# One f32r product a head for the relative-bias tables of a hybrid decoder layer

## The chip, the core and the metric

The kernel runs on one core of a Trainium2 chip. The metric is the device time of one execution in microseconds, as the median of several runs. A core has TensorE (PE; its weight loads are listed as PEld), VectorE (DVE), ScalarE (ACT), GpSimd (POOL) and SyncE (SP, whose queue issues all of this kernel's DMAs). Each engine runs its own instructions in a fixed order and waits on semaphores for the others.

## The reference

One decoder layer over 16 meta tokens and 1,024 tokens with 1,024 features: a norm and an input projection, four heads of differential attention beside four heads of a gated linear recurrence, an output projection, and a convolutional feed-forward part. The change concerns the bias of the attention scores alone:

```python
dist = q_pos[:, None] - k_pos[None, :]
bias = jnp.moveaxis(rel_table.astype(f32)[rel_bucket(dist)], -1, 0)
s = jnp.einsum('bhmqd,bhmkd->bhmqk', qblk, kh).astype(f32) * scale + bias[None, :, None]
s = jnp.where(dist >= 0, s, -jnp.inf)
```

`rel_table` has 32 buckets and 4 heads. The bucket depends on the distance alone, and all distances beyond a limit share one bucket, so a score needs its own bias only near the diagonal.

## The kernel before

All products that are to be exact are made in one of two ways. In plain f32, the program issues one matmul and the profile shows two records of it. Or an operand is split into a high part in f32r, a 4-byte type of reduced precision for TensorE, and a low part, also f32r, which is the rest; the projections multiply high by high, high by low and low by high (L203, L205, L207 in `proj_step`, and L847 in the first blocks). Writing a tile of type F32R rounds, and the rest is found by a subtraction.

The first 60 us do the following. The tokens come in blocks (`xt`), are scaled by their norm on DVE (`xs`, which needs the statistic `ss` of ACT), turned by PE (L242, into `px`) and split into `ahi` and `alo`. Beside that, PE makes the query, key and value projections of head 0 (`pi_dq`, `pi_dk`, `pi_dv`) for three groups of blocks. `smalls` and `lam_terms` make small vectors. The last group, `head0(2)`, is interleaved with `bias_tables`, which yields after each head, so that the four table products lie some 4 us apart among the projections.

`bias_tables` makes, for each head, 128 equal rows of 384 values: the bias at the distances 255 down to -128. The one-hot matrix `oh` (32 buckets by 384 distances, an input) is multiplied by `tbb`, which holds the 32 table values of a head, each repeated 128 times. The product of 128x384 goes to a bank `pb` in PSUM. DVE copies it to `rb`, subtracts its first column, POOL fills the last 128 columns with a large negative number, and SP stores it to `rsc` in DRAM. There is one `rb` buffer, so each head's copy waits until the store before has landed. `attn` then loads `rr` from `rsc` with a row step of 383, which shifts each row by one distance.

The order of PE's instructions is that of the program. On the other engines a scheduler sets it when the program is built. Each DMA waits for the one that held its lane before; lanes are taken in turn. The weights of the next stage (`wr_hf`, `wr_hq`, `wr_hi`, `wr_hg`, three buffers in all) are loaded by the same SP queue, split by ACT (`wh_...`) and POOL (`wl_...`). The next stage begins with the projection `pi_hf` and reuses the SBUF space of these first steps, for `kr` among others.

Most operations on DVE, ACT and POOL go through a helper, so that the profile gives L54 as their line; they are told apart by their tiles.

Of the kernel before, what the change touches and what calls it, by code (L numbers as in the profile page):

```python
# [9 lines left out]
F32 = mybir.dt.float32  # L10
F32R = mybir.dt.float32r
U8 = mybir.dt.uint8
AF = mybir.ActivationFunctionType
ALU = mybir.AluOpType
# [3 lines left out]
P = 128  # L18
# [7 lines left out]
HEADS = 4  # L26
# [60 lines left out]
def layer_kernel(ctx: ExitStack, tc: tile.TileContext, x, meta, table, lbl, gpre, gpost, win,  # L87
# [3 lines left out]
    V, A = Ordered(tc, nc.vector, state), Ordered(tc, nc.scalar, state)  # L91
    G = Ordered(tc, nc.gpsimd, state)
    T, SY = nc.tensor, nc.sync

    def pool(name, bufs, side="left", space=None):
        kw = {"side": side} if space is None else {"space": space}
        cm = tc.tile_pool(name=name, bufs=bufs, reuse_waits="tile", **kw)
        return cm, cm.__enter__()
# [42 lines left out]
    def ps_m(name):  # L141
        return pp.tile([P, 512], F32, tag="m", name=name, bufs=deep["m"])
# [43 lines left out]
    z_cm, zp = pool("pre", 2, "right")  # L186
# [105 lines left out]
        V.tensor_scalar(nlam, nlam, -(0.8 - 0.6 * math.exp(0.0)), None, ALU.add)  # L292

    def bias_tables():
        oh = zp.tile([32, 384], F32, tag="oh", name="oh", bufs=1)
        SY.dma_start(oh, onehot)
        tb = zp.tile([32, HEADS], F32, tag="tb", name="tb", bufs=1)
        SY.dma_start(tb, table)
        tbb = zp.tile([32, HEADS, P], F32, tag="tbb", name="tbb", bufs=1)
        V.tensor_copy(tbb, tb.rearrange("b (h o) -> b h o", o=1).to_broadcast([32, HEADS, P]))  # L300
        for h in range(HEADS):
            pt = ps_m(f"pb{h}")
            T.matmul(pt[:, :384], tbb[:, h], oh, start=True, stop=True)
            rb = zp.tile([P, 384], F32, tag="rb", name=f"rb{h}", bufs=1)
            V.tensor_copy(rb, pt[:, :384])
            V.tensor_scalar(rb[:, :256], rb[:, :256], rb[:, 0:1], None, ALU.subtract)
            G.memset(rb[:, 256:], NEG)
            SY.dma_start(rsc[h].rearrange("(p c) -> p c", p=P), rb)
            yield
# [604 lines left out]
    with tc.issue_after(last_lo.ins):  # L914
        smalls()
        lam_terms()
    interleave(head0(2), [bias_tables()], 2600)
    close(z_cm, p_cm)
    p_cm, pp = pool("ps", 2, space=PSUM)
# [722 lines left out]
```

## Time and profile before

| | |
|---|---|
| median of 3 runs | 1322.26 us (1322.09 to 1323.52) |
| the profiled execution | 1325.6 us |
| its span | 1323.8 us |
| granted TensorE clock, mean | 0.997 |
| busy: PE, DVE, ACT, POOL | 97%, 70%, 52%, 34% |

In a row of the timeline stand the start in us, the busy time, the engine, the line, the operation, the tile written and the tiles read, their shapes and the count; in brackets the idle time before it and what ended that. "SPq" is the issuing of a DMA. Ends of matmuls are modelled and overlap the next one, so the step from start to start is what a product costs PE. A stretch of the table of windows gives, after its length, the busy time and count of PE, PEld, DVE, ACT and POOL.

### The profile page before, as it was taken

What the parts mean: (1) busy time and instruction counts of PE and PEld (TensorE: products, weight loads), DVE (VectorE), ACT (ScalarE), POOL (GpSimd) and SP (SyncE); (2) the same over time, 40 slices, a digit from 0 to 9 for tenths busy, and PEclk for the clock granted to TensorE, in tenths of its full rate; (3) what the DMA queues carried; (4) which work ended last, traced back from release to release, by engine and by line L of the source; (5) the groups of instructions that cost most, each with busy time, mean ns of one, the idle gap of its engine ahead of it and who ended that gap; (6) DMA issues with size and microseconds to landing.
All of it is one profiled execution on the core that took longest, in us unless ns stands there. A gap on an engine that the chain in (4) does not pass through costs nothing.

```text
span 1323.8 us, 26191 instructions
## 1 busy us (share of the span) xinstructions
PE 1286.8 (97%) x10172; PEld 1185.5 (90%) x10172; DVE 930.1 (70%) x1531; ACT 692.5 (52%) x1635; POOL 455.4 (34%) x340
## 2 busy tenths in 40 slices
PE   8999999999999999899999999999999999999997
PEld 7899999899999988677999999999999997888875
DVE  6464646465645564547997788989989967697586
ACT  8475466547544754246754444444444435454553
POOL 5211211121112111243077667676676730010121
PEclk9999999999999999999999999999999999999999
DMA  5111121112111335487232234545445428865363
GB/s 209 61 40 33 54 57 41 49 46 65 44 42 41 88 101 169 153 277 254 81 112 80 80 95 154 177 144 173 154 144 166 144 84 275 312 205 166 88 206 120
DMA packets 99427, 165.00 MB, mean 125 GB/s; under 512 B 10035, under 2 KB 34899, under 8 KB 99302
## 3 DMA queue, kind: packets, MB, share of 16 engines
q1 hardware_dynamic: 99302, 163.32, 37.8%
q8 instruction: 80, 1.31, 0.4%
q14 instruction: 45, 0.37, 0.1%
HBM read 122.65 MB, written 40.63 MB: 123 GB/s over the span
## 4 chain that ended last, share of the span: by engine, by line
PE 45%; DVE 11%; ACT 3%; issue 3%; DMA 2%; POOL 0%; SPq 0%; DVEq 0%; ACTq 0%; POOLq 0%
PE pd L1491 5%; PE pd L1492 5%; PE pd L1490 5%; DVE c L54 5%; PE pb L1316 4%; PE pb L1317 3%; PE pb L1318 3%; PE pa L1316 2%; PE pa L1317 2%; PE pa L1318 2%; PE pc L1316 2%; PE pc L1317 2%; PE pc L1318 2%; PE py L976 1%; PE py L972 1%
## 5 line engine op out<-in xcount | busy, mean ns | idle before, releaser
L1316 PE MATMUL pb<-t,uh 128*128 128x258 f32 x504 | 144.0, 286 | 8.9 <-DVE u L54 8.9
L1318 PE MATMUL pb<-t,ul 128*128 128x258 f32 x504 | 141.6, 281 | 0.0
L1317 PE MATMUL pb<-t,uh 128*128 128x258 f32 x504 | 141.6, 281 | 0.0
L1491 PE MATMUL pd<-wl,gh 128*128 128x512 f32 x308 | 122.0, 396 | 1.2 <-DVE wl L54 1.1
L1492 PE MATMUL pd<-wh,gl 128*128 128x512 f32 x308 | 121.7, 395 | 0.0
L1490 PE MATMUL pd<-wh,gh 128*128 128x512 f32 x308 | 121.7, 395 | 0.0
L54 POOL TENSOR_TENSOR c<-c,c 128x514 f32<-128x514 f32 (+1 forms) x44 | 75.2, 1709 | 121.1 <-ACT c L54 111.4
L1316 PEld LDWEIGHTS pb<-t,uh 128*128 128x128 f32 x504 | 95.4, 189 | 12.2 <-DVE u L54 12.1
L54 DVE SCALAR_TENSOR_TENSOR c<-uu,cwt,c 128x514 f32<-128x514 f32 (+1 forms) x88 | 89.2, 1023 | 19.3 <-ACT c L54 19.0
L1317 PEld LDWEIGHTS pb<-t,uh 128*128 128x128 f32 x504 | 95.6, 190 | 0.0
L1318 PEld LDWEIGHTS pb<-t,ul 128*128 128x128 f32 x504 | 95.2, 189 | 0.0
L1316 PE MATMUL pa<-t,uh 128*128 128x258 f32 (+1 forms) x336 | 95.2, 283 | 0.0
L1318 PE MATMUL pa<-t,ul 128*128 128x258 f32 (+1 forms) x336 | 95.0, 283 | 0.0
L1317 PE MATMUL pa<-t,uh 128*128 128x258 f32 (+1 forms) x336 | 94.8, 282 | 0.0
L1316 PE MATMUL pc<-t,uh 128*128 128x258 f32 (+1 forms) x336 | 94.4, 281 | 0.0
L1317 PE MATMUL pc<-t,uh 128*128 128x258 f32 (+1 forms) x336 | 94.0, 280 | 0.0
L1318 PE MATMUL pc<-t,ul 128*128 128x258 f32 (+1 forms) x336 | 93.7, 279 | 0.0
L54 DVE SCALAR_TENSOR_TENSOR c<-ug,cwt,c 128x514 f32<-128x514 f32 (+1 forms) x88 | 89.6, 1019 | 0.9 <-ACT c L54 0.6
L54 ACT CAST uh<-ra 128x512 fp32r<-128x512 f32 x67 | 41.0, 616 | 66.4 <-PE pb L1317 48.2
L1491 PEld LDWEIGHTS pd<-wl,gh 128*128 128x128 f32 x308 | 57.7, 187 | 16.5 <-DVE wl L54 2.7
L54 POOL TENSOR_TENSOR ul<-ws,uh 128x512 fp32r<-128x512 f32 x42 | 64.7, 1541 | 20.4 <-ACT uh L54 20.4
L1492 PEld LDWEIGHTS pd<-wh,gl 128*128 128x128 f32 x308 | 57.7, 187 | 14.4 <-DVE gl L54 0.4
(373 smaller groups left out, 4161.2 us busy)
## 6 DMA issues: line engine op xcount, KB each, us to landing
ra<-in_wup_dram SPq DMA_DIRECT2D x88, 256.0 KB, 3.0
mp<-msc SPq DMA_DIRECT2D x23, 512.0 KB, 6.0
wd<-in_wdown_dram SPq DMA_DIRECT2D x44, 256.0 KB, 3.3
tsc<-wd SPq DMA_DIRECT2D x44, 256.0 KB, 3.2
wi<-tsc SPq DMA_DIRECT2D x44, 256.0 KB, 2.9
gi<-gsc SPq DMA_DIRECT2D x33, 256.0 KB, 4.1
wi<-in_wdown_dram SPq DMA_DIRECT2D x33, 256.0 KB, 5.3
gsc<-c SPq DMA_DIRECT2D x22, 257.0 KB, 2.3
```

What stands on the lines that cost most here:

```text
L54: ins = call(*args, **kw)
L972: T.matmul(py[:r], mh, hi, start=(first and k == ks[0]), stop=False)
L976: T.matmul(py[:r], ml, hi, start=False, stop=(last and k == ks[-1]))
L1316: T.matmul(pt, hi[:, s], th[:, k], start=(first and k == 0), stop=False, skip_group_check=True)
L1317: T.matmul(pt, hi[:, s], tl[:, k], start=False, stop=False, skip_group_check=True)
L1318: T.matmul(pt, lo[:, s], th[:, k], start=False, stop=(k == 3), skip_group_check=True)
L1490: T.matmul(py, gh[:, s], wh, start=(k == 0 and pr not in (3, 7)), stop=False, skip_group_check=True)
L1491: T.matmul(py, gh[:, s], wl, start=False, stop=False, skip_group_check=True)
L1492: T.matmul(py, gl[:, s], wh, start=False, stop=(k == NH - 1), skip_group_check=True)
```

## The change

The 32 table values become 64 rows: the f32r rounding of the values in rows 0 to 31, and what the rounding left out in rows 32 to 63. The one-hot matrix stands twice below itself, in f32r (its zeros and ones are exact). One product over 64 rows adds the two halves. For this, the one-hot matrix and the table are each loaded twice, the former into a plain f32 tile `ohr` that takes the buffer of `rb`; ACT copies it to f32r; DVE writes `tbb` over 64 rows as f32r and then overwrites rows 32 to 63 with the difference.

```diff
     def bias_tables():
-        oh = zp.tile([32, 384], F32, tag="oh", name="oh", bufs=1)
-        SY.dma_start(oh, onehot)
-        tb = zp.tile([32, HEADS], F32, tag="tb", name="tb", bufs=1)
-        SY.dma_start(tb, table)
-        tbb = zp.tile([32, HEADS, P], F32, tag="tbb", name="tbb", bufs=1)
-        V.tensor_copy(tbb, tb.rearrange("b (h o) -> b h o", o=1).to_broadcast([32, HEADS, P]))
+        oh = zp.tile([64, 384], F32R, tag="oh", name="oh", bufs=1)
+        raw = zp.tile([P, 384], F32, tag="rb", name="ohr", bufs=1)[:64]
+        tb = zp.tile([64, HEADS], F32, tag="tb", name="tb", bufs=1)
+        for l in range(2):
+            SY.dma_start(raw[32 * l:32 * l + 32], onehot)
+            SY.dma_start(tb[32 * l:32 * l + 32], table)
+        tbb = zp.tile([64, HEADS, P], F32R, tag="tbb", name="tbb", bufs=1)
+        A.copy(oh, raw)
+        tbr = tb.rearrange("b (h o) -> b h o", o=1)
+        V.tensor_copy(tbb, tbr.to_broadcast([64, HEADS, P]))
+        V.tensor_tensor(tbb[32:], tbr[32:].to_broadcast([32, HEADS, P]), tbb[32:].bitcast(F32), op=ALU.subtract)
         for h in range(HEADS):
             pt = ps_m(f"pb{h}")
             T.matmul(pt[:, :384], tbb[:, h], oh, start=True, stop=True)
```

The order of PE stays as it is. On DVE the two instructions stand among those of the small terms, ahead of the scaling `xs` of block 6:

```order
 L54 TENSOR_TENSOR lv<-lv 128x64
-L54 COPY tbb<-tb 32x512
+L54 COPY tbb<-tb 64x512
 L54 TENSOR_REDUCE le<-lv 128x1
+L54 TENSOR_TENSOR tbb<-tb,tbb 32x512
 L54 TENSOR_SCALAR xs_427<-xt_171,ss_428,gb 128x512 x2
```

The copy is wider, and the subtraction is new, behind a reduction of `lam_terms`. In SP's queue, the loads for the tables stand between those of the small vectors and the first weights of the next stage; before:

```order
L296 DMA oh<-in_onehot_dram 32x384
L298 DMA tb<-in_table_dram 32x4
L156 DMA wr_hf_0_726<-in_win_dram 128x512
L156 DMA wr_hf_1_732<-in_win_dram 128x512
L156 DMA wr_hq_0_738<-in_win_dram 128x512
```

and after:

```order
L299 DMA ohr<-in_onehot_dram 32x384
L300 DMA tb<-in_table_dram 32x4
L299 DMA ohr<-in_onehot_dram 32x384
L300 DMA tb<-in_table_dram 32x4
L156 DMA wr_hf_0_731<-in_win_dram 128x512
L156 DMA wr_hf_1_737<-in_win_dram 128x512
L156 DMA wr_hq_0_743<-in_win_dram 128x512
```

Two loads are added. Later in the same queue, the stores of the second to fourth table (`rsc`) alternate with weight loads; before:

```order
L308 DMA rsc<-rb_619 128x384
L156 DMA wr_hi_0_934<-in_win_dram 128x512
L308 DMA rsc<-rb_648 128x384
L156 DMA wr_hi_1_940<-in_win_dram 128x512
L156 DMA wr_hg_0_1147<-in_win_dram 128x512
L308 DMA rsc<-rb_679 128x384
```

and after:

```order
L313 DMA rsc<-rb_624 128x384
L156 DMA wr_hi_0_939<-in_win_dram 128x512
L156 DMA wr_hi_1_945<-in_win_dram 128x512
L313 DMA rsc<-rb_653 128x384
L156 DMA wr_hg_0_1152<-in_win_dram 128x512
L313 DMA rsc<-rb_684 128x384
```

The third table's store changes places with the load of `wr_hi_1`. With it, the third table's memset moves behind the split `wl_hq_0` on POOL, and on DVE the fourth table's copy moves behind the two `kl`. On ACT the copy of the one-hot matrix is added, ahead of the first copy to `avn`. Behind the four tables the order of every engine is the same as before.

## The prediction

> **What bounds the kernel now.** I read the page first, then the busy time in stretches, then the timeline of each engine round the bias tables, because all that the change touches lies in the first 60 us.
>
> ```profile
> span 1323.8 us, 26191 instructions
> ...
> PE 1286.8 (97%) x10172; PEld 1185.5 (90%) x10172; DVE 930.1 (70%) x1531; ACT 692.5 (52%) x1635; POOL 455.4 (34%) x340
> ...
> PE 45%; DVE 11%; ACT 3%; issue 3%; DMA 2%; POOL 0%; SPq 0%; DVEq 0%; ACTq 0%; POOLq 0%
> ```
>
> PE is busy for 97% of the span, and it holds most of what the page can place of the chain that ended last. The stretch table (busy time of PE, PEld, DVE, ACT, POOL, each with its count, then clock, DMA share and rate) says whether that holds where the tables are made:
>
> ```profile
> 42.36:59.62 17.26, 17.26 (x85) 14.05 (x85) 6.13 (x13) 6.20 (x12) 7.22 (x10) 1.00 0.35 114
> 59.62:460.00 400.38, 395.85 (x3884) 381.36 (x3883) 227.90 (x520) 229.57 (x675) 71.12 (x72) 1.00 0.17 49
> ```
>
> From 42.36 to 59.62 us, where the four table products stand between projections, PE is never idle, at full clock, and DVE, ACT and POOL work about a third of the time. In the 400 us behind it PE idles 4.5 us in all. So PE time saved before 59.62 moves everything behind it, unless a wait of another engine takes its place.
>
> The timeline of PE shows what a table product costs. L303 is the product; its "x2" are two records, since a plain f32 product runs as two. L203, L205 and L207 are projections in f32r, one record each.
>
> ```profile
> 42.19 0.34 PE L205 MATMUL pi_dv<-alo,w 128*128 128x384 f32 x1
> 42.36 0.34 PE L207 MATMUL pi_dv<-ahi,w 128*128 128x384 f32 x1
> 42.63 0.91 PE L303 MATMUL pb<-oh,tbb 32*128 32x384 f32 x2
> 43.47 0.45 PE L203 MATMUL pi_dq<-ahi,wh_dq 128*128 128x384 f32 x1
> 43.75 0.34 PE L205 MATMUL pi_dq<-alo,wh_dq 128*128 128x384 f32 x1
> ...
> 54.74 0.34 PE L207 MATMUL pi_dv<-ahi,w 128*128 128x384 f32 x1
> 55.00 0.91 PE L303 MATMUL pb<-oh,tbb 32*128 32x384 f32 x2
> 55.84 0.45 PE L203 MATMUL pi_dv<-ahi,w 128*128 128x384 f32 x1
> 56.12 0.34 PE L205 MATMUL pi_dv<-alo,w 128*128 128x384 f32 x1
> ```
>
> Busy times overlap here, so starts are what counts. Between f32r neighbours a 384-column product takes 0.17 to 0.18 us from start to start (42.19 to 42.36); I use 0.175. Round L303 the three steps from 42.36 to 43.75 take 1.39 us, and from 54.74 to 56.12 1.38 us, where three f32r steps would take 0.525. The excess has two parts: the two f32 records, and a stop at each end (42.36 to 42.63 is 0.27, not 0.175; 43.47 to 43.75 is 0.28).
>
> **The change part by part.**
>
> *The product on PE.* Four heads take 4 x 1.385 = 5.54 us now. If the single f32r product over 64 rows steps like its neighbours, they take 4 x 0.525 = 2.10, a gain of 3.44 us. Whether the stops go too is the open term, since no f32r product with fewer than 128 rows is in the trace. The nearest rows are products on other parts of the array:
>
> ```profile
> 66.30 0.34 PE L207 MATMUL pi_hf<-ahi,wl_hf 128*128 128x384 f32 x1
> 66.57 0.18 PE L670 MATMUL pt<-ident,pb 16*16 16x16 f32 x1
> 66.68 0.44 PE L203 MATMUL pi_hf<-ahi,wh_hf 128*128 128x384 f32 x1
> 66.96 0.33 PE L205 MATMUL pi_hf<-alo,wh_hf 128*128 128x384 f32 x1
> ...
> 135.36 0.28 PE L205 MATMUL pi_dq<-alo,wh_dq 128*128 128x272 f32 x1
> 135.57 0.73 PE L399 MATMUL pd<-hq,kr 128*32 128x32 f32 x62
> ...
> 535.60 0.39 PE L974 MATMUL py<-wol,mp 128*128 128x512 f32 x1
> 535.83 0.40 PE L976 MATMUL py<-woh,mp 128*128 128x512 f32 x1
> 536.07 0.40 PE L972 MATMUL py<-woh,m 128*2 128x512 f32 x1
> 536.30 0.40 PE L974 MATMUL py<-wol,m 128*2 128x512 f32 x1
> ```
>
> L670 (16 rows) and L399 (32 weight columns), both plain f32, are entered with the same stop: 0.27 us behind a 384-column step, 0.21 behind a 272-column one, against 0.175 and 272/384 of it, 0.124. L972 also uses a strip of the array (2 weight columns), but in f32r, and is entered without any: 0.24 and 0.23 against 0.23. So either the stop belongs to plain f32 on a part of the array, and goes; or it belongs to a part of the rows, and stays. The end of the bound where it stays comes from L670: 0.66 us from 66.30 to 66.96 with 16 columns, plus 368/384 of 0.175 = 0.17 for the other columns, is 0.83. The weight loads of the same rows differ:
>
> ```profile
> 66.57 0.08 PEld L670 LDWEIGHTS pt<-ident,pb 16*16 16x16 f32 x1 [0.26 <-issue]
> 66.68 0.19 PEld L203 LDWEIGHTS pi_hf<-ahi,wh_hf 128*128 128x128 f32 x1
> ```
>
> If a full load of 0.19 shows in place of the 0.08, it is 0.94. That is a gain of 0.45 to 0.56 per head, 1.8 to 2.2 us in all. I take 3.4: L399 and L972 are alike in tile and differ in type, which is just what the change alters.
>
> *DVE.* The copy of the table becomes a cast over 64 rows, and a subtraction over 32 rows is added behind it.
>
> ```profile
> 16.43 1.50 DVE L54 CAST w<-X_in 128x512 fp32r<-128x512 f32 x1
> ...
> 24.15 0.69 DVE L54 TENSOR_TENSOR alo<-px,ahi 128x512 fp32r<-128x512 f32 x1 [0.32 <-ACT ahi L54]
> ...
> 27.39 0.41 DVE L54 COPY tbb<-tb 32x512 f32<-32x512 f32 x1
> ...
> 29.47 1.41 DVE L54 SCALAR_TENSOR_TENSOR xs<-xt,ss,gb 128x512 f32<-128x512 f32 x2 [1.54 <-ACT ss L54]
> ```
>
> The cover is the 1.54 us for which DVE waits for ss of ACT in front of xs. A cast taken at 0.75 (half of the row at 16.43, the only f32r cast of this size on DVE, made beside POOL work, while POOL is idle at 27.39) adds 0.34, the subtraction 0.69: 1.03 us, hidden, with 0.5 to spare. With 1.50 for the cast and twice 0.69 for the subtraction it is 2.5 us, 0.9 past the cover; xs feeds the transposes of PE at 30.37, which wait as long. So 0 to +0.9 us; I take 0.
>
> *ACT.* The copy of the one-hot matrix, 64x384, is queued behind the two Exp of the small terms and ahead of avn.
>
> ```profile
> 33.60 0.52 ACT L54 COPY avn<-pn_va 16x128 f32<-16x128 f32 x2 [0.24 <-PE pn_va L319]
> 35.45 0.59 ACT L54 CAST ahi<-px 128x512 fp32r<-128x512 f32 x1 [1.34 <-PE px L242]
> ```
>
> At no more than the 0.59 of the 128x512 cast it fills the 0.24 and pushes avn by 0.35, which the 1.34 us wait ahead of ahi takes up: nothing. Without that cover it would cost PE 0.35.
>
> *SP and the DMAs.* Two more small loads stand ahead of the first weights of the next stage.
>
> ```profile
> 17.67 0.33 SPq L296 DMA_DIRECT2D oh<-in_onehot_dram  x1
> 19.13 0.33 SPq L298 DMA_DIRECT2D tb<-in_table_dram  x1
> 19.55 0.84 SPq L156 DMA_DIRECT2D wr_hf<-in_win_dram  x2
> ...
> 46.20 0.62 ACT L54 CAST wh_hf<-wr_hf 128x512 fp32r<-128x512 f32 x1
> ```
>
> At 1.46 us each (17.67 to 19.13) they move wr_hf to 22.5 at the latest; it is read at 46.20. Nothing.
>
> *The order behind the tables.* The memset of the third table now stands behind a weight split of POOL, its store behind a weight load of SP, and the fourth table's copy behind kl on DVE. The names end in rsc, which head 0 reads first, and in the freeing of the one rb buffer.
>
> ```profile
> 53.00 1.29 POOL L54 TENSOR_TENSOR wl_hq<-wr_hq,wh_hq 128x512 fp32r<-128x512 f32 x1 [0.20 <-ACT wh_hq L54]
> ...
> 58.05 0.33 SPq L308 DMA_DIRECT2D rsc<-rb  x1
> ...
> 63.61 0.40 ACT L54 ACTIVATE kr<-pi_hf 128x272 f32<-128x272 f32 x1
> ```
>
> The four stores of rb take this long from issue to landing:
>
> ```profile
> DMA to landing us min/median/max: 2.4/2.4/2.4
> ```
>
> With PE ahead by 1.7 us at the third table, that split ends near 52.6, so the memset and the store stay near where they are, and the last store, now at 58.05, leaves by about 57 and has landed at 59.4. The first big tile of the next stage, kr, may share the space of rb and would be written at 60.2 instead of 63.61, so 0.8 us are left. Nothing; if that margin were gone, the late part would hold ACT, and PE only behind it. What is next late is again PE.
>
> Sum: 3.4 us off the span, 1323.8 to 1320.4. The profiled execution took 1325.6, 1.8 outside the span, so it would read 1322.2. The median of the three runs, 1322.26, lies 3.3 below that execution; the same 3.4 off it gives 1318.9.
>
> **The rivals.**
>
> *The stops stay* (gain 1.8 to 2.2, middle 2.0: 1320.3). For it: L303 itself and L670, the only row-limited products, both stop. Against it: L399 stops with all 128 rows, and L972 does not. The Trainium skill, on the page TensorEngine Tiling, section Key Properties, says that a change of tiling mode, not merely of tile, drains TensorE. By that rule the gain would be this rival's; L303 agrees with it (0.27 us in place of 0.175), L972 does not (0.24 in place of 0.23).
>
> *The product does not get cheaper* (1322.3, up to 1323.2 with the 0.9 of DVE): 64 rows in f32r could run at the f32 pace. L972 speaks against it, at the full f32r step on a strip.
>
> *The second loads land late, and the kernel is slower.* DVE takes its work in order, so the cast of the table holds up xs, and xs holds up PE. The loads go out by 22.0 us at 1.46 apart. The cover is gone when the table lands after about 28.0 (29.47 less the 1.44 of cast and subtraction); from there each us costs PE one, and from 31.4 on the 3.4 us gain is used up. A landing at 35 us gives 1322.26 - 3.4 + 7.0 = 1325.9. Against it: from 22.0 to 28.0 are 6.0 us for a load of half a kilobyte.
>
> **How the numbers follow.** Forecast 0.55, stops stay 0.30, no cheaper 0.08, late loads 0.07. About 0.2%, 2.6 us, is what a measurement of this kernel can tell from no change, and the three runs span 1.4 us. The forecast's 3.4 is beyond 2.6 in about five of six cases, the 2.0 in one of four: faster 0.55 x 0.84 + 0.30 x 0.25 = 0.54; slower 0.07; the rest, 0.39, within. The range runs from 1317.7 (1.2 below the forecast, for the spread of runs) to 1321.7 (the small end of the gain with stops, 1320.5, and the same spread); it leaves out the last two rivals and the tails, 0.19.
>
> **What would show it.** In the changed profile: one record a table product; the three steps round it at 0.53 us if I am right, at 0.8 to 0.95 if the stops stay, near 1.4 if it is no cheaper. The first hf projection starts near 56.2 in place of 59.62 (57.6 with stops), and PE stays without idle time up to there. At 30.4 the transposes must not wait for xs. If all that holds and the span has not shrunk by as much, the gain was lost behind 60 us, which I hold for unlikely because all orders there stay as they are.

## The result and the profile after

| | before | after |
|---|---|---|
| median, 22 runs each | 1322.33 us (1321.17 to 1324.61) | 1320.38 us (1318.45 to 1323.21) |
| the profiled execution | 1325.6 us | 1319.7 us |
| its span | 1323.8 us | 1317.9 us |

The changed kernel takes 0.9985 of the time before (95% interval 0.9979 to 0.9992), 1.95 us less. The interval ends below 1, so that is faster, at about half of the forecast gain; the gain is less than the 2.6 us that the prediction took as the least that can be told from no change.

The page after (span; busy time of each engine) shows the same bound:

```profile
span 1317.9 us, 26191 instructions
...
PE 1282.9 (97%) x10168; PEld 1183.6 (90%) x10168; DVE 933.3 (71%) x1532; ACT 693.2 (53%) x1636; POOL 456.4 (35%) x340
```

PE has four records fewer, one for each table product. The timeline of PE after, round the first table product (now L308) and at the first projection of the next stage:

```profile
42.42 0.34 PE L207 MATMUL pi_dv<-ahi,w 128*128 128x384 f32 x1
42.69 0.44 PE L308 MATMUL pb<-oh,tbb 64*128 64x384 f32 x1
43.05 0.45 PE L203 MATMUL pi_dq<-ahi,wh_dq 128*128 128x384 f32 x1
43.34 0.34 PE L205 MATMUL pi_dq<-alo,wh_dq 128*128 128x384 f32 x1
...
57.76 0.29 PE L203 MATMUL pi_hf<-ahi,wh_hf 128*128 128x272 f32 x1
```

The two records have become one, but the stops are still there: the three steps take 0.27, 0.36 and 0.29 us (42.42 to 42.69, to 43.05, to 43.34), where a plain step is 0.175. The three steps from L207 to L205 take 0.92 us; over the four heads they are 0.92, 0.93, 0.91 and 0.91, 3.67 us in all, where it was 5.54. That is a gain of 1.87. The first hf projection starts at 57.76 in place of 59.62, 1.86 us earlier.

The weight loads of the same place show what a stop is:

```profile
42.24 0.19 PEld L207 LDWEIGHTS pi_dv<-ahi,w 128*128 128x128 f32 x1
42.68 0.18 PEld L308 LDWEIGHTS pb<-oh,tbb 64*128 64x128 f32 x1 [0.25 <-issue]
43.05 0.19 PEld L203 LDWEIGHTS pi_dq<-ahi,wh_dq 128*128 128x128 f32 x1 [0.18 <-issue]
```

The load for L207 starts at 42.24, 0.18 us ahead of its matmul, under the one before. The load for the table product starts at 42.68, together with its matmul, after 0.25 us in which the loader did nothing; the load for the L203 behind it waits in the same way. So going into the table product and coming out of it, PE gives up the overlap of load and matmul.

In the stretches between the table products and behind them (busy time and count of PE, PEld, DVE, ACT, POOL, then clock, DMA share and rate), PE stays the bound:

```profile
42.42:57.76 15.34, 15.34 (x82) 13.56 (x81) 6.95 (x12) 6.19 (x12) 6.26 (x9) 1.00 0.39 115
57.76:460.00 402.24, 397.70 (x3896) 383.15 (x3896) 230.80 (x525) 230.81 (x678) 71.96 (x74) 1.00 0.17 49
...
545.00:550.00 5.00, 5.00 (x30) 4.30 (x30) 0.99 (x3) 1.11 (x3) 0.00 (x0) 1.00 0.00 0
```

It is never idle up to 57.76, and idles 4.54 us from there to 460, against 4.53 before from 59.62 on. What was gained at the tables is carried on whole.

The two profiled spans differ by 5.9 us, three times as much. I don't put the rest down to the change: it arises behind 460 us, where the order of both programs is the same, and one part of it can be seen in the same stretch of the execution before:

```profile
545.00:550.00 5.00, 5.00 (x27) 3.47 (x26) 2.29 (x4) 0.58 (x1) 0.00 (x0) 0.66 0.30 108
```

Its granted clock fell to 0.66 there. Runs of one kernel lie some us apart (the table above): the execution profiled before lies 3.3 us above the median of its kernel, the one after 0.7 below. So one pair of profiles cannot tell 2 us; the medians of 22 runs can, and their 1.95 agrees with the 1.87 of the steps.

### The profile page after: what moved, and what is told of

Its sections match the earlier page's. It is cut to its first block, busy times and chain, and to the rows that moved or that the text cites. A ratio compares the mean times of both kernels' runs of the same rounds, so it can differ in the third digit from the quotient of the medians.

```text
span 1317.9 us, 26191 instructions
## 1 busy us (share of the span) xinstructions
PE 1282.9 (97%) x10168; PEld 1183.6 (90%) x10168; DVE 933.3 (71%) x1532; ACT 693.2 (53%) x1636; POOL 456.4 (35%) x340
## 4 chain that ended last, share of the span: by engine, by line
PE 45%; DVE 10%; issue 3%; ACT 2%; DMA 2%; POOL 1%; SPq 0%; DVEq 0%; ACTq 0%; POOLq 0%
PE pd L1496 5%; PE pd L1497 5%; PE pd L1495 5%; DVE c L54 4%; PE pb L1321 4%; PE pb L1322 4%; PE pb L1323 4%; PE pa L1321 2%; PE pa L1323 2%; PE pa L1322 2%; PE pc L1321 2%; PE pc L1322 2%; PE pc L1323 2%; PE py L981 1%; PE py L977 1%
```

## Experiments

The theory after the result: a product that uses fewer than the 128 rows of the array stops PE on the way in and out, whatever its type, and plain f32 costs more on top. The rivals: the stop depends on the type (and 64 rows in f32r have some other cost), it depends on how few rows there are, or it is nothing but the weight load standing free. The experiments e1 to e4 were timed beside the kernel before, whose median over 32 runs was 1321.83 us there; e5 and e6 were run once each and are read from the steps alone.

**e1: 128 rows, f32r.** The changed kernel with rows 64 to 127 of both operands filled with zeros:

```diff
-        oh = zp.tile([64, 384], F32R, ...)
-        raw = zp.tile([P, 384], F32, tag="rb", name="ohr", bufs=1)[:64]
-        tb = zp.tile([64, HEADS], F32, ...)
+        oh = zp.tile([P, 384], F32R, ...)
+        raw = zp.tile([P, 384], F32, tag="rb", name="ohr", bufs=1)
+        tb = zp.tile([P, HEADS], F32, ...)
+        G.memset(raw[64:], 0.0)
+        G.memset(tb[64:], 0.0)
...
-        tbb = zp.tile([64, HEADS, P], F32R, ...)
+        tbb = zp.tile([P, HEADS, P], F32R, ...)
...
-        V.tensor_copy(tbb, tbr.to_broadcast([64, HEADS, P]))
-        V.tensor_tensor(tbb[32:], ...)
+        V.tensor_copy(tbb, tbr.to_broadcast([P, HEADS, P]))
+        V.tensor_tensor(tbb[32:64], ...)
```

> The changed kernel with its 64 rows filled up to 128 by rows of zeros in both operands, so that the f32r product covers the whole array. Rows theory (a product over fewer than 128 rows makes PE stop on entry and on exit, whatever its type): the three steps round a table product fall from 0.92 to about 0.53 us, the first hf projection starts near 56.2 us in place of 57.76, and the time is 1.5 us below the changed kernel and 3.4 below the one before (ratio 0.9974). Lone-product theory (any single product with operands of its own between projections stops PE, rows or not): the steps stay at 0.92 and the time at the changed kernel's.

The timeline of PE in e1 (the table product is L310):

```profile
42.58 0.34 PE L207 MATMUL pi_dv<-ahi,w 128*128 128x384 f32 x1
42.76 0.34 PE L310 MATMUL pb<-oh,tbb 128*128 128x384 f32 x1
42.93 0.34 PE L203 MATMUL pi_dq<-ahi,wh_dq 128*128 128x384 f32 x1
43.11 0.33 PE L205 MATMUL pi_dq<-alo,wh_dq 128*128 128x384 f32 x1
...
56.40 0.29 PE L203 MATMUL pi_hf<-ahi,wh_hf 128*128 128x272 f32 x1
```

and of its weight loads:

```profile
42.59 0.19 PEld L310 LDWEIGHTS pb<-oh,tbb 128*128 128x128 f32 x1
42.76 0.19 PEld L203 LDWEIGHTS pi_dq<-ahi,wh_dq 128*128 128x128 f32 x1
```

The three steps take 0.53 us, a table product steps like any projection, and its load runs under the matmul before. In the product nothing but the number of rows differs from the changed kernel, so the stops belong to the rows. The time is 1318.61 us (10 runs), 0.9977 of before (0.9968 to 0.9987): 3.2 us less, about what the prediction expected of the change itself. The two memsets on POOL cost nothing that shows. By median it is the fastest of the kernels here. It is faster than the kernel before; that it is faster than the changed kernel is shown by the steps alone, since the two intervals (0.9968 to 0.9987 here, 0.9979 to 0.9992 there) overlap.

**e2: 128 rows, plain f32.** The kernel before with its 32 rows filled up to 128 with zeros:

```diff
-        oh = zp.tile([32, 384], F32, ...)
-        tb = zp.tile([32, HEADS], F32, ...)
+        oh = zp.tile([P, 384], F32, ...)
+        tb = zp.tile([P, HEADS], F32, ...)
+        G.memset(oh, 0.0)
+        G.memset(tb, 0.0)
+        SY.dma_start(oh[:32], onehot)
+        SY.dma_start(tb[:32], table)
...
-        tbb = zp.tile([32, HEADS, P], F32, ...)
+        tbb = zp.tile([P, HEADS, P], F32, ...)
```

> The kernel before, in plain f32, with its 32 rows filled up to 128 by zeros; neither split nor f32r. Rows theory: the stops go and the two f32 records stay, so the three steps take 0.175 on entry, about 0.66 for the two records, and 0.26 for the step behind (as behind the plain f32 products of the value step in the profile before), 1.1 us in place of 1.39: 1.1 us less than before in all (ratio 0.9992). Type theory, on which the forecast rested (the stop belongs to plain f32 on a part of the array): the same 1.1, since the part is gone. Lone-product theory: 1.39 as before.

The timeline of PE in e2:

```profile
42.43 0.34 PE L207 MATMUL pi_dv<-ahi,w 128*128 128x384 f32 x1
42.60 0.81 PE L305 MATMUL pb<-oh,tbb 128*128 128x384 f32 x2
42.95 0.63 PE L203 MATMUL pi_dq<-ahi,wh_dq 128*128 128x384 f32 x1
43.42 0.34 PE L205 MATMUL pi_dq<-alo,wh_dq 128*128 128x384 f32 x1
```

0.99 us for the three steps, where 1.1 was expected. L305 is entered after 0.17, without a stop, though it is plain f32. What is above 0.525, 0.465, is the price of plain f32: the two records take 0.35 from start to start, and the step behind them 0.47 in place of 0.175. With 32 rows the same product took 1.385, so the rows cost 0.395 there. The time, 1320.86 us (11 runs), is 0.9991 of before (0.9982 to 1.0000), which agrees with the expected 0.9992; the interval reaches 1, so the time alone does not settle it, and the steps do.

**e3: 32 rows, f32r.** The changed kernel with the high halves alone; the low halves of the table are left out, so it computes less:

```diff
-        oh = zp.tile([64, 384], F32R, ...)
-        tb = zp.tile([64, HEADS], F32, ...)
-        for l in range(2): ...
-        tbb = zp.tile([64, HEADS, P], F32R, ...)
+        oh = zp.tile([32, 384], F32R, ...)
+        tb = zp.tile([32, HEADS], F32, ...)
+        SY.dma_start(raw, onehot)
+        SY.dma_start(tb, table)
+        tbb = zp.tile([32, HEADS, P], F32R, ...)
...
-        V.tensor_tensor(tbb[32:], ...)
```

> The f32r product over 32 rows: the low halves of the table values are left out, so this part of the bias is only as precise as f32r. Type alone is changed against the kernel before. Rows theory: 0.92 us for the three steps, as with 64 rows, and the changed kernel's time. Type theory: 0.53. If the stop grows with the number of rows that are loaded or not loaded, it differs from 0.92.

The timeline of PE in e3:

```profile
42.34 0.34 PE L207 MATMUL pi_dv<-ahi,w 128*128 128x384 f32 x1
42.61 0.43 PE L305 MATMUL pb<-oh,tbb 32*128 32x384 f32 x1
42.98 0.44 PE L203 MATMUL pi_dq<-ahi,wh_dq 128*128 128x384 f32 x1
43.26 0.34 PE L205 MATMUL pi_dq<-alo,wh_dq 128*128 128x384 f32 x1
```

0.92 us, as with 64 rows: 32 rows stop PE no more than 64 do, and f32r doesn't spare it. Its time, 1321.23 us (11 runs), 0.9993 (0.9984 to 1.0003), settles nothing, since the interval holds both no change and the 0.9985 of the changed kernel; the steps do.

With these, the three steps round a table product are:

| rows | plain f32 | f32r |
|---|---|---|
| 32 | 1.385 (before) | 0.92 (e3) |
| 64 | | 0.92 (after) |
| 128 | 0.99 (e2) | 0.53 (e1) |

The two costs add up: 0.39 for 32 or 64 rows in place of 128, in either type, 0.465 for plain f32 at either number of rows.

**e4: the four products together.** The changed kernel with the four products issued back to back, ahead of the loop:

```diff
+        pts = [ps_m(f"pb{h}") for h in range(HEADS)]
+        for h in range(HEADS):
+            T.matmul(pts[h][:, :384], tbb[:, h], oh, start=True, stop=True)
         for h in range(HEADS):
-            pt = ps_m(f"pb{h}")
-            T.matmul(pt[:, :384], tbb[:, h], oh, start=True, stop=True)
+            pt = pts[h]
```

> The changed kernel with its four table products one behind the other, ahead of the first of the projections between which they stood. Rows theory (the cost is that of changing between 64 and 128 rows, not that of the product): one entry and one exit in place of four, so from the projection before to the second one behind about 0.92 + 3 x 0.18 = 1.45 us, and 1.2 us less than the changed kernel in all (ratio to before 0.9976). If each product pays for itself: four times what it pays now, no gain on the changed kernel.

The timeline of PE in e4 (one row for all four products):

```profile
42.31 0.34 PE L207 MATMUL pi_dv<-ahi,w 128*128 128x384 f32 x1
42.58 0.96 PE L308 MATMUL pb<-oh,tbb 64*128 64x384 f32 x4
43.47 0.45 PE L203 MATMUL pi_dq<-ahi,wh_dq 128*128 128x384 f32 x1
43.76 0.34 PE L205 MATMUL pi_dq<-alo,wh_dq 128*128 128x384 f32 x1
```

From L207 to L205 there are 1.45 us for six steps, which at 0.175 would take 1.05: one pair of stops, 0.40, instead of four. A row of products of the same kind doesn't stop between them, so it is the change between kinds that costs, and not the free-standing load of each. The time is 1319.02 us (11 runs), 0.9977 (0.9968 to 0.9986).

**e5 and e6: a strip of the columns.** The prediction had argued from column strips. e5 is e1 with one more product in front of each table product, over all 128 rows but with 32 weight columns; e6 is the same in plain f32:

```diff
             pt = ps_m(f"pb{h}")
+            T.matmul(pt[:32, :384], tbb[:, h, :32], oh, start=True, stop=True)                                   # e5
+            T.matmul(pt[:32, :384], tbb[:, h, :32].bitcast(F32), oh.bitcast(F32), start=True, stop=True)         # e6
             T.matmul(pt[:, :384], tbb[:, h], oh, start=True, stop=True)
```

> The kernel with 128 rows, with one more f32r product ahead of each table product: the same operands, but 32 weight columns in place of 128; its result is written over. Rows alone stop PE: four steps at 0.175, so 0.70 us from the projection ahead to the second one behind. A strip of columns stops it as a strip of rows does (and 2 weight columns were an exception): about 0.92 + 0.175 = 1.1 us.

> The same with the added product of 32 weight columns in plain f32. Type matters for columns (as the entry of the 32-column products of the recurrence in the profile before was read): a stop at each end, 1.39 + 0.175 = 1.56 us. Rows alone stop PE, and that entry has another cause, such as the short products themselves: 0.99 + 0.175 = 1.17 us.

The timeline of PE in e5 (L310 is the strip, L311 the table product):

```profile
42.19 0.34 PE L207 MATMUL pi_dv<-ahi,w 128*128 128x384 f32 x1
42.36 0.34 PE L310 MATMUL pb<-oh,tbb 128*32 128x384 f32 x1
42.54 0.34 PE L311 MATMUL pb<-oh,tbb 128*128 128x384 f32 x1
42.72 0.34 PE L203 MATMUL pi_dq<-ahi,wh_dq 128*128 128x384 f32 x1
42.89 0.33 PE L205 MATMUL pi_dq<-alo,wh_dq 128*128 128x384 f32 x1
```

and in e6:

```profile
42.51 0.34 PE L207 MATMUL pi_dv<-ahi,w 128*128 128x384 f32 x1
42.78 0.83 PE L310 MATMUL pb<-oh,tbb 128*32 128x384 f32 x2
43.54 0.44 PE L311 MATMUL pb<-oh,tbb 128*128 128x384 f32 x1
43.82 0.34 PE L203 MATMUL pi_dq<-ahi,wh_dq 128*128 128x384 f32 x1
44.00 0.34 PE L205 MATMUL pi_dq<-alo,wh_dq 128*128 128x384 f32 x1
```

In f32r the strip is one more step of 0.175 and nothing else: 0.70 us from L207 to L205. In plain f32 it is entered after 0.27, and the second step behind it takes 0.28; the four steps take 1.49 us, near the 1.56 expected with stops and far from the 1.17 without. So on 32 columns the stop does hang on the type, and such a strip has it in plain f32 alone; on rows it does not. In one run each beside 1321.56 us of the kernel before, e5 took 1320.07 us and e6 1320.77.

## Why the prediction was right or wrong

The time, 1320.38 us, lies in the range and on the forecast's side. It is the time of the rival in which the stops stay (1320.3), not of the likeliest case (1318.9). So the range held because it was drawn wide enough to take in that rival, to which the prediction gave a chance of 0.30, and not because the mechanism it held for likeliest was right.

*The step that failed* is "I take 3.4: L399 and L972 are alike in tile and differ in type". The pair was read rightly, and e5 and e6 show that on 32 columns the type decides. What failed is the carrying over from columns to rows: the rows of the profile had no f32r product with fewer than 128 rows, and after, e1, e2 and e3 show that the stop goes with the rows in both types. L670 and L303, which use few rows, were the nearer ones. On this the Trainium skill, on the page TensorEngine Tiling, section Key Properties, had the rule that a change of tiling mode drains TensorE: after, e3 and e4 agree with it (0.39 us for the way in and the way out together); e5 agrees only if a strip of 32 columns in f32r is no change of mode, which no run here shows (0.70 us for four steps, entered without a stop).

*The size of the rival* was right: 0.92 us for the three steps, within the forecast 0.83 to 0.94, and 1.87 us in all, within 1.8 to 2.2. Of the two ends, the full weight load was the better one, as the 0.18 of the load at 42.68 shows.

*That the gain would be carried on whole* was right: PE has no idle time up to 57.76 and as much as before behind it.

*DVE* was right that it is hidden, but less of the cover went than I said. The timeline of DVE after:

```profile
27.46 0.41 DVE L54 CAST tbb<-tb 64x512 fp32r<-64x512 f32 x1
...
28.03 0.68 DVE L54 TENSOR_TENSOR tbb<-tb,tbb 32x512 fp32r<-32x512 f32 x1
...
29.54 1.42 DVE L54 SCALAR_TENSOR_TENSOR xs<-xt,ss,gb 128x512 f32<-128x512 f32 x2 [0.82 <-ACT ss L54]
```

The cast took 0.41 us, as long as the copy over half the rows, and not 0.75; the subtraction took 0.68, as forecast. The wait for ss went from 1.54 to 0.82, so 0.8 us were to spare, and xs started at 29.54, against 29.47.

*ACT* went as worked out: the cast of the one-hot matrix took 0.50 us (0.59 was the bound), and ACT still waited 1.29 us ahead of ahi, against 1.34. Its timeline after:

```profile
33.31 0.50 ACT L54 CAST oh<-ohr 64x384 fp32r<-64x384 f32 x1
...
35.52 0.59 ACT L54 CAST ahi<-px 128x512 fp32r<-128x512 f32 x1 [1.29 <-PE px L242]
```

*The loads* moved the first weights by 1.1 us, not by up to 2.9, and the tables held nothing up: the cast started at 27.46, where the copy had started at 27.39. The last store, though, went the wrong way. The issues of SP's queue after:

```profile
20.66 0.84 SPq L156 DMA_DIRECT2D wr_hf<-in_win_dram  x2
...
44.24 0.33 SPq L313 DMA_DIRECT2D rsc<-rb  x1
46.11 0.33 SPq L603 DMA_DIRECT2D rr<-rsc  x1
...
58.58 0.33 SPq L313 DMA_DIRECT2D rsc<-rb  x1
```

I had it leave by 57; it left at 58.58, later than the 58.05 before, though PE was 1.86 us ahead. What it waited for stands in the next rows: DVE's and POOL's timelines; last, ACT's first write of `kr`.

```profile
51.54 0.56 DVE L54 COPY rb<-pb 128x384 f32<-128x384 f32 x1 [0.60 <-DMA rsc<-rb]
52.13 1.07 DVE L54 TENSOR_SCALAR rb<-rb 128x256 f32<-128x256 f32 x1
...
56.54 0.56 DVE L54 COPY rb<-pb 128x384 f32<-128x384 f32 x1 [0.74 <-DMA rsc<-rb]
57.14 1.37 DVE L54 TENSOR_SCALAR rb<-rb 128x256 f32<-128x256 f32 x1
```

```profile
51.62 1.29 POOL L54 TENSOR_TENSOR wl_hq<-wr_hq,wh_hq 128x512 fp32r<-128x512 f32 x1 [1.36 <-ACT wh_hq L54]
```

```profile
61.76 0.40 ACT L54 ACTIVATE kr<-pi_hf 128x272 f32<-128x272 f32 x1
```

The single `rb` had become the chain to watch. The copies of the third and fourth table now wait 0.60 and 0.74 us for the store before to land, and the subtraction of the first column took 1.07 and 1.37 us in place of 0.37. The last store left right behind the 1.37 (57.14 to 58.51).

The prediction also misread how long a store takes: the 2.4 us is the landing of one store, the second, and not of all four. By the semaphore events of the traces, the first and the last store land 1.85 us after their issue in both kernels (after, the first lands at 46.09, and the load `rr` that waits for it, L603, leaves at 46.11). The second and the third took 2.4 and 1.85 us before, and 3.2 and 3.1 after, where each leaves some 0.4 us behind a weight load; that the loads are the reason is not tested. So the last store after landed at 60.43, 1.3 us ahead of `kr` at 61.76, and in e1, which had the gain of 3.4 us, at 58.44, 2.0 us ahead of `kr` at 60.40. `kr` follows its projection by 4.0 us in both, as before (59.62 to 63.61). So nothing was lost here, and no run shows whether `kr` waits for that store at all.

## What to carry to other kernels

A product over 32 or 64 of the 128 contraction rows, alone among full ones, cost PE a stop on the way in and out that its own duration doesn't show: price it by the steps from start to start including its neighbours, and either fill the rows up to 128 with zeros or put such products side by side. Before a behaviour is carried from one row of the trace to another, ask in which dimension they are alike: here a strip of columns and a strip of rows behaved differently. When a saving pulls a bound engine ahead, look at each single buffer beside it, whose store and refill don't get faster.

## What the runs showed of the hardware

- Rows of the array: 0.39 us for the way in and the way out together of products with 32 or 64 rows among products with 128, in f32 and f32r alike, between 384-column products at full clock; none with rows of zeros up to 128. Columns: none for 32 columns in f32r, a stop in plain f32.
- A plain f32 product over 384 columns costs 0.465 us more than one in f32r, by the three steps round it, with 32 rows (before and e3) and with 128 (e2 and e1).
- DVE was held up beside POOL. After, the subtraction on `rb` started at 52.13, in the middle of POOL's split (51.62 to 52.91), and ended at 53.20, 0.29 behind it. In e1 the same pair came in nearly the same order, but the subtraction met the end of the split and took its usual time, by the rows of DVE and POOL:

```profile
51.86 0.38 DVE L54 TENSOR_SCALAR rb<-rb 128x256 f32<-128x256 f32 x1
```

```profile
50.64 1.29 POOL L54 TENSOR_TENSOR wl_hq<-wr_hq,wh_hq 128x512 fp32r<-128x512 f32 x1 [0.97 <-ACT wh_hq L54]
```

In e3 and e5 it ended 0.28 and 0.29 us behind the split too, after 1.10 and 0.78 us: the earlier it began within the split, the longer it took. The copy out of PSUM just ahead of it (51.54 in after) ran beside the same split and took its usual 0.56. The fourth subtraction ran beside a memset of POOL (`am`): it took 1.37 us in after, e5 and e6, with 1.06 for the memset, and 0.38 in e1, e3 and e4, with 1.21 for the memset. It began 0.02 to 0.03 us ahead of POOL's row of memsets each time, so the starts don't tell which engine is held up.

The Trainium skill, on the page SBUF — State Buffer, section SBUF: two separate sides, says that the two engines share a pair of ports, which for some kinds of DVE instruction one of them holds for a whole instruction while the other blocks. The 1.07 us agree with that, if the subtraction is of such a kind. No experiment was made for this, so it is a reading of traces and not a test.
